# A hybrid decoder trunk on one core: the program issued in the order of its own list schedule

## The chip, the cores and the metric

The kernel runs on one core of a Trainium2 chip. The metric is the device time of one execution in microseconds. The kernel before took 1468.79 us, the median of three runs (1468.52 to 1474.27).

## The reference

Two layers on a sequence of 1024 rows and a width of 1024, in float32. Layer A is differential attention, layer B stick-breaking attention; each mixer's output is multiplied by a SiLU gate before its output projection, and added to the residual.

```
def _diff_attention(...):            # layer A, 8 heads, causal
    def probs(qb, k):
        s = einsum('bhqd,bshd->bhqs', qb, k) * scale
        return softmax(where(mask, s, -inf))
    a = probs(qb1, k1) - lam * probs(qb2, k2)
    return einsum('bhqs,bshe->bhqe', a, v)

def _stick_breaking(q, k, v):        # layer B, 16 heads of 64
    z = einsum('bhqd,bshd->bhqs', qb, k) * scale
    log_beta = log_sigmoid(z)
    log_1mb = where(mask, log_sigmoid(-z), 0.0)
    suffix = cumsum(log_1mb, reverse=True) - log_1mb
    a = where(mask, exp(log_beta + suffix), 0.0)
    return einsum('bhqs,bshe->bhqe', a, v)

x = x + (rms(diff_attention(...)) * (1 - lambda_init) * silu(g)) @ w_out      # layer A
x = x + (stick_breaking(...) * silu(g)) @ w_out                               # layer B
```

## The kernel before, in words

Every projection runs as three matmuls, because each operand is split into a high and a low part: high x high, high x low, low x high (L223 to L225; names `ah`/`al` for activations, two `w` tiles for weights). `group` (L211 on) makes such a projection in steps; a projection is 256 or 512 columns wide and accumulates into a PSUM tile `proj`, of which there are two.

Layer A treats its heads one after the other, layer B pairs of heads. For a head the program makes the projections of q, k, v and the gate; `scores` (L257 on) makes one visit of `sc` (one buffer of two banks, 64-row matmuls) for one or two blocks of 128 query rows; a chain on VectorE and ScalarE turns each score row tile `zl` into weights (layer A: L671 to L687; layer B: L855 copy, L857 mask on GpSimd, L867, two activations, L870, the scan L872, L873); `transposed` (L303 on) transposes them in TensorE into `tr` (three buffers), ScalarE copies that to `th` (L319), VectorE writes the rest to `tl` (L320), and the `av` matmuls read `th` and `tl` (L702 to L704, L888, L889) into the one `av` buffer, which L712 or L894 and L895 empty.

While head h is in its attention, the projections of head h+1 fill TensorE: `merge` interleaves the two lists of steps by their weights in the program's text. During layer A the weights of layer B are also converted and written back to DRAM: `park` (L178 on) loads a 256 KB `raw` tile, ScalarE makes `ph` from it (L186, L189), VectorE the rest (L187, L190), and two DMAs store them. At the start, `norm_rows` (L125 on) normalizes each of eight blocks of 128 rows: a Square with a sum on ScalarE (L129), some short instructions, a scale on VectorE (L131), eight transposes (L136), and the split into `ah` and `al` (L140, L141); the weights of the first head are split beside it (L162 to L165). Sixteen warm-up matmuls (L110) stand in front.

The order in which instructions reach each engine's queue is not that of the text. The tile framework collects them, and places them by a list schedule of its own with a timing model of the simulator; `hp()` puts an instruction ahead of all others, `later()` 400 places back. Each engine then works its queue strictly in order and waits on semaphores, and all DMAs of the kernel stand in the one queue of SyncE. The order is asked for in one line:

```
    with tile.TileContext(nc, schedule_with_timeline_sim=True) as tc:
        build(tc, args, out)
```

Of the kernel before, what the change touches and what calls it, by code (L numbers as in the profile page):

```python
# [34 lines left out]

def build(tc, ins, out):
    nc = tc.nc
    act, dve, pool, pe = nc.scalar, nc.vector, nc.gpsimd, nc.tensor
# [16 lines left out]
    layer_pool = lctx.enter_context(tc.tile_pool(name="la", bufs=1))  # L55
    def hp(k="hpe"):
# [5 lines left out]
    act.preload_act_table_set("natural_log_exp_and_others")  # L62
# [5 lines left out]
    layer = [layer_pool, 0]  # L68

    def T(tag, shape, bufs, dt=F32, pool=None):  # L70
        n_t[0] += 1
        return (pool or sb).tile(shape, dt, tag=tag, bufs=bufs, name=f"{tag}_{n_t[0]}")

    def PS(tag, bufs):
        n_t[0] += 1
        return ps.tile([P, 512], F32, tag=tag, bufs=bufs, name=f"{tag}_{n_t[0]}")
# [16 lines left out]
    def C(name, shape, dt=F32):  # L93
        return cp.tile(shape, dt, name=name)
# [3 lines left out]
    make_identity(nc, ident)  # L98
    eps = C("eps", [P, 1])
    dve.memset(eps, EPS)  # L100
    ones = layer_pool.tile([P, P], F32, name="ones")
    pool.memset(ones, 1.0 / P)
    mask_a = layer_pool.tile([P, HALF], mybir.dt.bfloat16, name="mask_a")
# [42 lines left out]
    def split_w(dst, src, gain=None):  # L146
# [3 lines left out]
        with hp("hpw") if len(started) > 1 else ExitStack():  # L150
            raw = T("raw", [P, HALF], B["raw"], pool=layer[0]) if started else T("o", [P, HALF], B["o"])
            r3 = raw.rearrange("p (k n) -> p k n", k=k)
            nc.sync.dma_start(raw if len(src.shape) == 2 else raw.rearrange("p (k n) -> p k n", k=src.shape[1]), src)
# [24 lines left out]
    def park(src, gain, dst):  # L178

        with later():  # L180
# [3 lines left out]
            nc.sync.dma_start(raw, src)  # L184
# [6 lines left out]
            for i, t in enumerate((f32(h), raw)):  # L191
                nc.sync.dma_start(dst(i), t.rearrange("p (j n) -> p j n", j=2))

    def w_parked(src):

        ws = [w_slots(4, 256) for _ in range(2)]
        for g in range(2):
            for i in range(2):
                nc.sync.dma_start(f32(ws[g][i]).rearrange("p k n -> p (k n)"), src[i, :, g * 1024:(g + 1) * 1024])
# [11 lines left out]
    def group(n, pairs, done):  # L211
# [45 lines left out]
    def scores(hd, visit, evac):  # L257

        first = True
        n_t[0] += 1  # L260
        pts = ps.tile([P, 2, 512], F32, tag="sc", bufs=1, name=f"sc_{n_t[0]}")
        col = 0
        for i, off, w in visit:
            rs_ = slice((i % 4) * P, (i % 4) * P + P)
            q, wm = hd.q[i // 4], max(w, 256)
# [698 lines left out]
```

## Time and profile before

| | |
|---|---|
| median of three runs | 1468.79 us |
| the profiled execution | 1470.76 us |
| its span, first to last instruction | 1469.0 us |
| granted TensorE clock, mean | 0.988 |
| PE busy | 1392.2 us |
| DVE, ACT, POOL busy | 1072.0, 908.8, 303.3 us |

PE is TensorE, DVE VectorE, ACT ScalarE, POOL GpSimd, SP the queue that issues DMAs. A matmul's end is modelled, so PE counts as busy while one is in its pipeline. Length less PE busy is the time in which TensorE did nothing. The granted clock is a share of 2.4 GHz; the engine has two levels, 1.2 and 2.4, so a share between them is a mixture. An instruction's idle time is the gap on its engine before it, and the name behind the arrow is what ended the gap.

### The profile page before, as it was taken

To read this page: it belongs to the slowest core of one execution; us is meant where nothing else is said; L and a number is where in the kernel's file an instruction comes from. 1 tells how busy PE (TensorE), PEld (TensorE's weight loads), DVE (VectorE), ACT (ScalarE), POOL (GpSimd) and SP (SyncE) were. 2 spreads that over 40 slices of the span, in tenths; PEclk is the share of its full clock that TensorE was granted. 3 is DMA by queue.
4 is the path that set the end of the run, shared out by engine and by line. 5 is a ranking of instruction groups with operands and counts; after the bars stand their busy time and mean duration, and the time that the engine had idled before them with its cause. 6 is when DMAs were issued, how large, how long until landed. Compare 5 with 4: busy or idle time off the path is not lost.

```text
span 1469.0 us, 24737 instructions
## 1 busy us (share of the span) xinstructions
PE 1392.2 (95%) x8944; PEld 1172.3 (80%) x8944; DVE 1072.0 (73%) x2145; ACT 908.8 (62%) x1834; POOL 303.3 (21%) x545
## 2 busy tenths in 40 slices
PE   8999999999989897899999999999999999988899
PEld 8888888888878786779987877777777877777799
DVE  8677787888777867886425786877878686788851
ACT  7666666666656656554226677768677676787610
POOL 0102112111221212110002232223314242334200
PEclk9999999999999999999999999999999999999999
DMA  5156555546455625351522122111212121253624
GB/s 202 62 161 209 155 193 185 169 151 212 151 172 172 194 83 190 112 205 73 179 73 87 63 68 63 69 58 63 80 58 87 58 87 58 72 194 137 229 84 147
DMA packets 94602, 185.93 MB, mean 127 GB/s; under 512 B 8720, under 2 KB 43792, under 8 KB 93456
## 3 DMA queue, kind: packets, MB, share of 16 engines
q1 hardware_dynamic: 94480, 184.35, 37.6%
q8 instruction: 71, 1.16, 0.3%
q14 instruction: 51, 0.42, 0.1%
HBM read 119.31 MB, written 65.01 MB: 125 GB/s over the span
## 4 chain that ended last, share of the span: by engine, by line
PE 40%; DVE 24%; ACT 13%; issue 11%; DMA 8%; POOL 2%; SPq 0%; ACTq 0%; DVEq 0%; POOLq 0%
PE proj L223 10%; PE proj L224 9%; PE proj L225 9%; DVE u4k L872 6%; DVE u4k L870 4%; PE tr L313 3%; PE sc L269 2%; ACT u4k L868 2%; DVE u4k L867 2%; DVE tl L320 2%; ACT u4k L869 2%; DVE zl L671 2%; ACT zl L682 2%; PE av L888 2%; DMA w_kv<-raw 1%
## 5 line engine op out<-in xcount | busy, mean ns | idle before, releaser
L223 PE MATMUL proj<-ah,w 128*128 128x512 f32 x768 | 309.9, 404 | 0.0
L225 PE MATMUL proj<-ah,w 128*128 128x512 f32 x768 | 308.0, 401 | 0.0
L224 PE MATMUL proj<-al,w 128*128 128x512 f32 x768 | 307.6, 400 | 0.0
L223 PE MATMUL proj<-w,ah 128*128 128x256 f32 x992 | 284.3, 287 | 9.5 <-ACT qk L610 6.2
L224 PE MATMUL proj<-w,ah 128*128 128x256 f32 x992 | 280.8, 283 | 0.0
L225 PE MATMUL proj<-w,al 128*128 128x256 f32 x992 | 280.7, 283 | 0.0
L223 PEld LDWEIGHTS proj<-w,ah 128*128 128x128 f32 x992 | 187.9, 189 | 18.4 <-ACT qk L610 8.4
L224 PEld LDWEIGHTS proj<-w,ah 128*128 128x128 f32 x992 | 188.0, 189 | 3.2 <-issue 2.5
L225 PEld LDWEIGHTS proj<-w,al 128*128 128x128 f32 x992 | 187.7, 189 | 1.9 <-issue 1.8
L872 DVE TENSOR_TENSOR_SCAN u4k<-zl,u4k 128x768 f32<-128x768 f32 (+4 forms) x96 | 182.1, 1903 | 1.2
L320 DVE TENSOR_TENSOR tl<-tr,th 128x512 fp32r<-128x512 f32 (+1 forms) x240 | 146.4, 628 | 43.3 <-ACT th L319 38.6
L225 PEld LDWEIGHTS proj<-ah,w 128*128 128x128 f32 x768 | 144.7, 188 | 35.3 <-issue 5.5
L223 PEld LDWEIGHTS proj<-ah,w 128*128 128x128 f32 x768 | 144.6, 188 | 34.2 <-issue 4.9
L224 PEld LDWEIGHTS proj<-al,w 128*128 128x128 f32 x768 | 144.9, 189 | 32.5 <-issue 4.2
L269 PE MATMUL sc<-kh,q 64*128 64x512 f32 (+2 forms) x768 | 141.3, 385 | 11.6 <-DVE small L671 10.6
L313 PE MATMUL tr<-ident,zl 128*128 128x128 f32 x864 | 131.3, 279 | 19.9 <-DVE tl L320 12.0
L873 ACT ACTIVATE zl<-u4k 128x768 f32<-128x768 f32 (+4 forms) x96 | 81.3, 846 | 107.4 <-DVE u4k L872 83.2
L857 POOL TENSOR_SCALAR_AFFINE_SELECT zl<-zl 128x128 f32<-128x128 f32 (+1 forms) x96 | 92.8, 980 | 236.6 <-ACT zl L855 223.3
L319 ACT ACTIVATE th<-tr 128x512 fp32r<-128x512 f32 (+1 forms) x240 | 126.3, 553 | 24.0 <-PE tr L313 17.3
L313 PEld LDWEIGHTS tr<-ident,zl 128*128 128x128 f32 x864 | 101.6, 143 | 38.9 <-DVE tl L320 18.3
L870 DVE SCALAR_TENSOR_TENSOR u4k<-zl,u4k 128x768 f32<-128x768 f32 (+4 forms) x96 | 94.1, 997 | 48.2 <-ACT u4k L869 47.7
L682 ACT ACTIVATE zl<-zl,small 128x256 f32<-128x256 f32 (+7 forms) x128 | 98.0, 768 | 29.2 <-DVE small L681 20.7
(150 smaller groups left out, 2547.0 us busy)
## 6 DMA issues: line engine op xcount, KB each, us to landing
w<-w_kv SPq DMA_DIRECT2D x32, 512.0 KB, 5.2
w<-w_b SPq DMA_DIRECT2D x32, 512.0 KB, 5.0
w<-w_o SPq DMA_DIRECT2D x24, 512.0 KB, 4.9
raw<-in_w_kv_dram SPq DMA_DIRECT2D x32, 256.0 KB, 2.9
w_kv<-ph SPq DMA_DIRECT2D x32, 256.0 KB, 3.1
w_kv<-raw SPq DMA_DIRECT2D x32, 256.0 KB, 3.4
raw<-in_w_b_dram SPq DMA_DIRECT2D x32, 256.0 KB, 3.0
w_b<-ph SPq DMA_DIRECT2D x32, 256.0 KB, 3.0
```

Of the source, the lines that this page charges most:

```text
L223: pe.matmul(box["p"], lh, rh, start=(j == 0), stop=False)
L224: pe.matmul(box["p"], lh, rl, start=False, stop=False)
L225: pe.matmul(box["p"], ll, rh, start=False, stop=last)
L269: pe.matmul(pts[:, c, col:col + wm], q[a][HI[c], rs_], hd.k[b][HI[c], off:off + wm], start=(a + b == 0), stop=(a == 1))
L313: pe.transpose(pt[:, o:o + P], a[:, (2 * t + b) * P:(2 * t + b + 1) * P], ident)
L319: act.activation(th[:, skip:], pt[:, skip:], AF.Copy)
L320: dve.tensor_tensor(tl[:, skip:], pt[:, skip:], f32(th[:, skip:]), ALU.subtract)
L682: act.activation(p[c][:, :n], p[c][:, :n], AF.Exp, bias=b, scale=-1.0, accum_out=s[:, c:c + 1])
L857: pool.affine_select(t3[:, :, n - P:], t3[:, :, n - P:], [[0, len(cs)], [-1, P]], ALU.is_ge, -BIG, base=-1, channel_multiplier=1)
L870: dve.scalar_tensor_tensor(u, zc, 0.0, u, ALU.min, ALU.subtract)
L872: dve.tensor_tensor_scan(ur, t[:, 1:w2 + 1][:, ::-1], ur, 0.0, ALU.add, ALU.subtract)
L873: act.activation(zc, u, AF.Exp, scale=-1.0)
```

## The change

The calls to the engines no longer go to the framework at once. `Order` records each with its engine, its operands and a duration from a table (`cost`), and at the end `issue` runs a list schedule: whenever an engine is free it takes the ready instruction of the lowest priority number (the place in the text; `hp()` goes ahead of all, `later()` 400 places back), if the buffers that it needs are free. The framework then only gets the instructions in that order. The three matmuls of a projection step, and all matmuls of one score visit, are recorded as one entry (`together`). Which instructions there are, their operands and the buffers are unchanged. All instructions carry the line of the one place that issues them, L374.

```
+class L:                                   # an operand: a tile and the part of it that is used
+    def part(self):
+        if self.root.space == "dram":
+            return self.box or [(0, n) for n in self.root.shape]
+        lo, hi = int(self.idx.min()), int(self.idx.max()) + 1
+        if self.root.space == "psum":
+            return [(lo // 512, (hi + 511) // 512)]
+        return [self.p, (lo, hi)]
...
+    def add(self, eng, method, a, kw):
+        took, lag = self.cost(eng, method, a, kw)
+        if eng == "pe" and not self.cur and a[1].p[1] - a[1].p[0] == 64:
+            took += 0.42
...
+            op.prio = i - 10 ** 9 if self.shift is None else i + self.shift
...
+        for x, w in [(x, False) for x in ins] + [(x, True) for x in outs]:
+            r, part = x.root, x.part()
+            for other, opart in (r.writes + r.reads if w else r.writes):
+                if other is not op and all(p[0] < q[1] and q[0] < p[1] for p, q in zip(part, opart)):
+                    op.deps.add(other)
...
+    def cost(self, eng, method, a, kw):
...
+        if eng == "pe":
...
+            t = {512: 0.228, 384: 0.172, 256: 0.12}[n]
+            return (t / 2, 0.17) if a[1].p[1] - a[1].p[0] == 64 else (t, 0.17)
...
+        if eng == "act":
+            by = isinstance(kw.get("scale"), L)
+            return (0.18 if by else 0.08) + (0.00078 if psum else 0.00086) * n + (0.19 if "accum_out" in kw else 0), 0.17
+        if eng == "dve":
+            if method == "tensor_tensor_scan":
+                return 0.06 + 0.0021 * n, 0.15
...
+        size = (k.p[1] - k.p[0]) * int(np.prod(k.idx.shape)) * 4
+        return 0.07, size / 180e3
...
+    def issue(self, prepare):
...
+                    op.at, free[e] = now, now + op.took
+                    if e == "sp":
+                        dma = max(now + 1.2, dma) + op.lag
+                        end = dma + 0.8
+                    else:
+                        end = free[e] + op.lag
...
+        with self.tc.manual_schedule():
+            for op in order:
...
+                e = self.real[op.eng]
+                for method, a, kw in op.calls:
+                    getattr(e, method)(*[real(x) for x in a], **{k: real(v) for k, v in kw.items()})
...
-    act, dve, pool, pe = nc.scalar, nc.vector, nc.gpsimd, nc.tensor
+    rec = Order(tc, {"pe": nc.tensor, "act": nc.scalar, "dve": nc.vector, "pool": nc.gpsimd, "sp": nc.sync})
+    act, dve, pool, pe, sp = (rec.engine(e) for e in ("act", "dve", "pool", "pe", "sp"))
...
     def hp(k="hpe"):
-        return tc.high_priority(offset=None if B[k] < 0 else B[k])
+        return rec.priority(None)
 
     def later():
-        return tc.high_priority(offset=-B["late"])
+        return rec.priority(B["late"])
...
-                pe.matmul(box["p"], lh, rh, start=(j == 0), stop=False)
-                pe.matmul(box["p"], lh, rl, start=False, stop=False)
-                pe.matmul(box["p"], ll, rh, start=False, stop=last)
+                with rec.together():
+                    pe.matmul(box["p"], lh, rh, start=(j == 0), stop=False)
+                    pe.matmul(box["p"], lh, rl, start=False, stop=False)
+                    pe.matmul(box["p"], ll, rh, start=False, stop=last)
...
+    rec.issue(prepare)
```

Three places show what moved. The first is ScalarE's queue in layer A, where the q and k projections of head 6 (of 0 to 7) begin: `ph` is a conversion of a parked weight, `qk` the evacuation of a projection. Before:

```order
L189 ACTIVATE ph_5819<-raw_5818,cols 128x512
L710 ACTIVATE t1k_4975<-tr_4977,eps 128x256
L291 ACTIVATE q_965_5036<-tr_5031,cols 128x512
L711 ACTIVATE t1k_4975<-t1k_4975 128x256
L291 ACTIVATE kh_5013<-tr_5040,cols 128x512
L189 ACTIVATE ph_5871<-raw_5870,cols 128x512
L610 ACTIVATE qk_5812<-proj_5787 128x256
L319 ACTIVATE th_5178<-tr_5174 128x384
L189 ACTIVATE ph_5937<-raw_5936,cols 128x512
L189 ACTIVATE ph_6042<-raw_6041,cols 128x512
L610 ACTIVATE qk_5812<-proj_5841 128x256
L707 ACTIVATE t1k_5190<-av_5173 128x256
```

and now, from shortly after the first `qk` evacuation of that head to the third:

```order
L374 ACTIVATE th_5819<-tr_5781 128x512
L374 ACTIVATE o_5826<-g2k_5716 128x512
L374 ACTIVATE o_5826<-o_5826 128x512 x2
L374 ACTIVATE qk_5788<-proj_5790 128x256
L374 ACTIVATE w_5753<-raw_5772,cols 128x256 x2
L374 ACTIVATE g1k_5868<-qk_5788 128x256
L374 ACTIVATE th_5874<-tr_5845 128x512
L374 ACTIVATE w_5882<-raw_5778,cols 128x256 x2
L374 ACTIVATE th_5897<-tr_5857 128x512
L374 ACTIVATE w_5882<-raw_5832,cols 128x256 x2
L374 ACTIVATE ph_5937<-raw_5880,cols 128x512
L374 ACTIVATE qk_5788<-proj_5864 128x256
```

Before, four conversions stand in ten rows, two of them straight in front of a `qk` evacuation; now one does, and the rows between are splits of the next weights, copies of transposes and the gate.

The second is TensorE's queue at the start. Each pair of `tr` rows is one block of x's rows (blocks 0 and 1 before; 0 is not repeated below), `proj` the first projection, of block 0. Before:

```order
L136 MATMUL tr_126<-ident,zl_112 128x128 x4
L136 MATMUL tr_133<-ident,zl_112 128x128 x4
L223 MATMUL proj_460<-w_140,ah_105 128x256
L224 MATMUL proj_460<-w_141,ah_105 128x256
L136 MATMUL tr_184<-ident,zl_170 128x128 x4
L136 MATMUL tr_191<-ident,zl_170 128x128 x4
L225 MATMUL proj_460<-w_140,al_106 128x256
L223 MATMUL proj_460<-w_140,ah_105 128x256
L224 MATMUL proj_460<-w_141,ah_105 128x256
L225 MATMUL proj_460<-w_140,al_106 128x256
```

and now, from the first projection on (`proj_195` is of block 0, `proj_245` of block 1):

```order
L374 MATMUL proj_195<-w_166,ah_182 128x256
L374 MATMUL proj_195<-w_171,ah_182 128x256
L374 MATMUL proj_195<-w_166,al_189 128x256
L374 MATMUL tr_224<-ident,zl_210 128x128 x4
L374 MATMUL tr_232<-ident,zl_210 128x128 x4
L374 MATMUL proj_245<-w_166,ah_182 128x256
L374 MATMUL proj_245<-w_171,ah_182 128x256
L374 MATMUL proj_245<-w_166,al_189 128x256
L374 MATMUL tr_263<-ident,zl_228 128x128 x4
L374 MATMUL tr_275<-ident,zl_228 128x128 x4
L374 MATMUL tr_286<-ident,zl_251 128x128 x4
L374 MATMUL tr_296<-ident,zl_251 128x128 x4
```

Before, the rest of block 0's projection follows the transposes of block 1; now it follows those of block 3, and one triple of block 1 has moved ahead of blocks 2 and 3.

The third is TensorE's queue in layer B, from the last transpose of a group to the `av` matmuls that read it. Before (the `av` matmul that reads this group stands 14 projection matmuls and one score group behind the last row):

```order
L313 MATMUL tr_11726<-ident,zl_11467 128x128
L313 MATMUL tr_11742<-ident,zl_11390 128x128
L313 MATMUL tr_11742<-ident,zl_11468 128x128
L313 MATMUL tr_11742<-ident,zl_11390 128x128
L313 MATMUL tr_11742<-ident,zl_11468 128x128
L313 MATMUL tr_11771<-ident,zl_11390 128x128
L313 MATMUL tr_11771<-ident,zl_11468 128x128
L313 MATMUL tr_11771<-ident,zl_11390 128x128
L313 MATMUL tr_11771<-ident,zl_11468 128x128
L223 MATMUL proj_11797<-ah_8570,w_11203 128x512
L224 MATMUL proj_11797<-al_8571,w_11203 128x512
L225 MATMUL proj_11797<-ah_8570,w_11204 128x512
```

and now:

```order
L374 MATMUL tr_11832<-ident,zl_11263 128x128
L374 MATMUL sc_11836<-kh_10440,q_2108_10962 128x256 x2
L374 MATMUL sc_11836<-kl_10457,q_2108_10962 128x256 x2
L374 MATMUL sc_11836<-kh_10440,q_2109_10970 128x256 x2
L374 MATMUL sc_11836<-kh_10440,q_2108_10962 128x256 x2
L374 MATMUL sc_11836<-kl_10457,q_2108_10962 128x256 x2
L374 MATMUL sc_11836<-kh_10440,q_2109_10970 128x256 x2
L374 MATMUL av_11706<-th_11799,v_10775 128x256
L374 MATMUL proj_11795<-ah_8729,w_11152 128x512
L374 MATMUL proj_11795<-al_8740,w_11152 128x512
L374 MATMUL proj_11795<-ah_8729,w_11155 128x512
L374 MATMUL av_11706<-tl_11806,v_10775 128x256
```

The `av` matmul that reads `th` now stands one score group behind the transposes, and the one that reads `tl` a projection triple behind that.

## Rows read from the trace of the kernel before

**Rows 1.** The page, busy time of each engine: us (share of the span) x instructions.
```profile
PE 1392.2 (95%) x8944; PEld 1172.3 (80%) x8944; DVE 1072.0 (73%) x2145; ACT 908.8 (62%) x1834; POOL 303.3 (21%) x545
```

**Rows 2.** Busy time by stretch; columns: length, PE, PEld, DVE, ACT, POOL, PEclk, DMA, GB/s.
```profile
0.00:560.00 560.00, 537.24 (x3619) 464.62 (x3620) 427.38 (x1141) 361.30 (x842) 95.95 (x149) 0.99 0.51 165
560.00:605.00 45.00, 33.22 (x215) 25.60 (x214) 38.93 (x102) 26.52 (x59) 14.12 (x19) 0.92 0.51 176
605.00:745.00 140.00, 136.82 (x1042) 125.85 (x1041) 92.76 (x249) 61.24 (x137) 6.60 (x21) 1.00 0.39 134
745.00:1200.00 455.00, 443.22 (x2436) 347.32 (x2435) 327.88 (x402) 311.48 (x538) 122.73 (x238) 1.00 0.22 71
1200.00:1311.00 111.00, 101.71 (x574) 80.27 (x574) 86.66 (x111) 78.85 (x143) 35.55 (x64) 0.97 0.24 86
1311.00:1402.00 91.00, 76.11 (x529) 65.01 (x528) 80.34 (x105) 66.00 (x113) 27.64 (x52) 0.94 0.50 180
1402.00:1469.00 67.00, 63.85 (x542) 63.62 (x540) 18.03 (x40) 3.40 (x8) 0.71 (x4) 1.00 0.35 126
```

**Rows 3.** Waits of PE, whole span: waiting, releaser, us in total, times, longest.
```profile
PE tr L313 <- DVE tl L320: 12.0, 8, 4.0
PE av L888 <- DVE o L895: 11.0, 13, 2.7
PE sc L269 <- DVE small L671: 10.6, 10, 2.4
...
PE proj L223 <- ACT qk L610: 6.2, 7, 1.7
```

**Rows 4.** Waits of ACT in 0 to 600 us.
```profile
ACT ph L189 <- DMA raw<-in_w_kv_dram: 21.7, 17, 3.5
ACT ph L189 <- DMA raw<-in_w_b_dram: 17.9, 13, 3.6
```

**Rows 5.** Timeline of ACT from 420 us: start, length, instruction, idle before and releaser.
```profile
420.26 0.72 ACT L189 ACTIVATE ph<-raw,cols 128x512 fp32r<-128x512 f32 x1 [3.54 <-DMA raw<-in_w_b_dram]
420.89 0.36 ACT L610 ACTIVATE qk<-proj 128x256 f32<-128x256 f32 x1
```

**Rows 6.** The page, DMA issues: count, KB each, us to landing.
```profile
raw<-in_w_b_dram SPq DMA_DIRECT2D x32, 256.0 KB, 3.0
```

**Rows 7.** Timeline of ACT in the first 30 us.
```profile
6.22 2.51 ACT L164 ACTIVATE w<-o,cols 128x256 fp32r<-128x256 f32 x6 [0.28 <-DMA o<-in_w_qk_dram]
8.77 1.06 ACT L129 ACTIVATE zl<-kl 128x1024 f32<-128x1024 f32 x1
```

**Rows 8.** Timeline of PE in the first 30 us.
```profile
10.15 1.97 PE L136 MATMUL tr<-ident,zl 128*128 128x128 f32 x8 [2.09 <-DVE small L118]
...
12.64 1.50 PE L136 MATMUL tr<-ident,zl 128*128 128x128 f32 x8
13.90 0.36 PE L225 MATMUL proj<-w,al 128*128 128x256 f32 x1
...
23.11 1.03 PE L136 MATMUL tr<-ident,zl 128*128 128x128 f32 x8
```

**Rows 9.** Groups by shape: instruction, count, busy us, mean ns, idle before and releasers.
```profile
L320 DVE TENSOR_TENSOR tl<-tr,th 128x512 fp32r<-128x512 f32 x144 | 95.9, 683 | 26.6 <-ACT th L319 22.3 <-issue 3.1 <-PE tr L313 0.8
...
L320 DVE TENSOR_TENSOR tl<-tr,th 128x384 fp32r<-128x384 f32 x96 | 51.7, 546 | 16.8 <-ACT th L319 16.3
...
L319 ACT ACTIVATE th<-tr 128x512 fp32r<-128x512 f32 x144 | 82.1, 594 | 12.9 <-PE tr L313 8.5 <-PE av L888 2.3 <-POOL o L246 1.3
...
L872 DVE TENSOR_TENSOR_SCAN u4k<-zl,u4k 128x768 f32<-128x768 f32 x24 | 45.0, 1876 | 0.5
...
L872 DVE TENSOR_TENSOR_SCAN u4k<-zl,u4k 128x640 f32<-128x640 f32 x16 | 32.9, 2083 | 0.0
...
L867 DVE TENSOR_SCALAR u4k<-zl 128x896 int32<-128x896 int32 x16 | 16.2, 1049 | 4.5 <-ACT zl L855 4.4
...
L867 DVE TENSOR_SCALAR u4k<-zl 128x768 int32<-128x768 int32 x24 | 12.9, 538 | 6.6 <-POOL zl L857 6.6
```

More of the change, by code (lines that the diff above doesn't have):

```diff
@@ L1 @@
+import heapq
 import math
@@ new lines, in _rearranged, with groups @@
+def _rearranged(idx, pat, kw):
+    def groups(s):
+        out_, cur = [], None
+        for t in s.replace("(", " ( ").replace(")", " ) ").split():
+            if t == "(":
+                cur = []
+            elif t == ")":
+                out_.append(cur)
+                cur = None
+            elif cur is None:
+                out_.append([t])
+            else:
+                cur.append(t)
+        return out_
+    a, b = (groups(s) for s in pat.split("->"))
+    assert a[0] == b[0] == ["p"]
+    a, b = a[1:], b[1:]
+    size, names = dict(kw), []
+    for g, n in zip(a, idx.shape):
+        known = int(np.prod([size[t] for t in g if t in size]))
+        for t in g:
+            if t not in size:
+                size[t] = n // known
+        names += g
+    x = idx.reshape([size[t] for t in names])
+    order = [t for g in b for t in g]
+    return x.transpose([names.index(t) for t in order]).reshape([int(np.prod([size[t] for t in g])) for g in b])
@@ L66, in build, with fixed, kept @@
     n_w = [0]
-    layer = [layer_pool, 0]
+    layer = ["la", 0]
     def T(tag, shape, bufs, dt=F32, pool=None):
         n_t[0] += 1
-        return (pool or sb).tile(shape, dt, tag=tag, bufs=bufs, name=f"{tag}_{n_t[0]}")
+        pool, name = pool or "sb", f"{tag}_{n_t[0]}"
+        return L(Root(shape, dt, "psum" if pool == "ps" else "sbuf", pool, slot=(pool, tag), bufs=bufs,
+                      make=lambda: pools[pool].tile(shape, dt, tag=tag, bufs=bufs, name=name)))
     def PS(tag, bufs):
-        n_t[0] += 1
-        return ps.tile([P, 512], F32, tag=tag, bufs=bufs, name=f"{tag}_{n_t[0]}")
+        return T(tag, [P, 512], bufs, pool="ps")
+    def fixed(pool, shape, dt, name):
+        return L(Root(shape, dt, "sbuf", pool, real=pools[pool].tile(shape, dt, name=name)))
+    def kept(shape, name):
+        return L(Root(shape, F32, "dram", "dr", real=dr.tile(shape, F32, name=name)))
     zt = lambda: T("zl", [P, S], B["al"], pool=layer[0])
@@ L93, in C @@
     def C(name, shape, dt=F32):
[L94 removed]
+        return fixed("cp", shape, dt, name)
     ident = C("ident", [P, P])
[L98 removed]
+    make_identity(nc, ident.real())
     eps = C("eps", [P, 1])
     dve.memset(eps, EPS)
[L101 removed]
+    ones = fixed("la", [P, P], F32, "ones")
     pool.memset(ones, 1.0 / P)
[L103 removed]
+    mask_a = fixed("la", [P, HALF], mybir.dt.bfloat16, "mask_a")
     pool.memset(mask_a, 0.0)
@@ L805, in build, with prepare @@
               OutProj(ins["a_w_out"], og_a, x_in, heads_a, sink_a, {0: (0, D)}), (0, 1), extra)
-    lctx.close()
-    layer[1] = 1
-    layer[0] = lctx.enter_context(tc.tile_pool(name="lb", bufs=1))
+    layer[:] = ["lb", 1]
+    def prepare():
+        if "lb" not in pools:
+            lctx.close()
+            pools["lb"] = lctx.enter_context(tc.tile_pool(name="lb", bufs=1))
     def qkv_b(p):
```

295 lines of the change are left out of this document (256 added, 39 removed).

## The prediction, made before the changed kernel ran

> **What bounds the kernel now.** First the engines' totals [rows 1]: TensorE is busy 95% of a span of 1469.0 us, VectorE 73%, ScalarE 62%. An order can win only what TensorE stands still or runs slow, so the second view is the table of stretches [rows 2]. Length less PE busy is idle time: 22.8 us in 0 to 560 (layer A, heads 0 to 6), 11.8 in 560 to 605 (its last head), 3.2 in 605 to 745, 11.8 in 745 to 1200 (layer B, steady), 9.3 in 1200 to 1311, 14.9 in 1311 to 1402 (layer B's last heads), 3.1 in the tail: 76.8 in all. Where it idles the granted clock is under 1: 0.99, 0.92, 0.97 and 0.94. One less that share, times the length, is 5.6 + 3.6 + 3.3 + 5.5 = 18 us lost to time at 1.2 instead of 2.4 GHz. The two make 95 us, and start and end (about 7) stay, so 1380 is the least that reordering can reach.
>
> Third, what ended TensorE's waits [rows 3]: no DMA is among the releasers. It waits for ScalarE and VectorE to empty or fill a tile: `tl` 12.0 us, `o` 11.0, the row minima behind the scores 10.6, `qk` 6.2. Fourth, why those are late in layer A: ScalarE itself waits for loads of weights that it converts for layer B, 21.7 and 17.9 us [rows 4]. The stretch at 416 to 421 us shows how one becomes the other [rows 5]: conversion `ph` of L189 heads ScalarE's queue, its data arrive 3.54 us later, and only behind it comes L610, for which TensorE stands. In layer B the late ones are VectorE's, which works 80.3 of 91 us in the last stretch [rows 2].
>
> **The change part by part.** Instructions and their durations are the same on every engine; only places in the five queues change. I go stretch by stretch.
>
> Layer A, steady: 22.8 idle, of which about 4 is the first wait for data, leaving 18.8. The old order put four `ph` conversions into ten rows of ScalarE, around the first `qk` evacuations of a head; the new one has a single one in the twelve rows that hold the second and third (the first place shown). The cost table gives a 256 KB load 1.2 + 262,144 / 180,000 + 0.8 = 3.5 us and makes transfers queue behind each other; the trace has 3.0 from issue to landing [rows 6]. So a conversion is placed when its data are there, and what was a blocked queue becomes a few us of ordinary waits. I take back 15 of 18.8; bounds: 0 (the waits only move) and 18.8.
>
> Layer A, last head: 11.8 idle. Little filling work is left, and in the new order some score groups still stand directly behind one another. A score tile has one buffer, and two evacuations of 128x512 stand between two groups (`th` has the same form and takes 0.59 us [rows 9]), so with hand-overs about 1.5 us of idle each, some four times. I take back 5; bounds 0 and 8.
>
> Layer B, steady: 11.8 idle. At the third place shown the old order leaves 17 projection matmuls and more between a transpose and the first `av` matmul that reads it; the new one leaves a score group, and one projection triple between the readers of `th` and of `tl`. That costs nothing if ScalarE and VectorE are on time (0.59 + 0.68 us for the two halves [rows 9], 1.3 to 1.6 with hand-overs), and it gives buffers back earlier. The table is right for most shapes but not all: it has 0.06 + 0.0021 x 640 = 1.40 us for the scan of 640, the trace 2.08 [rows 9]. The extra 0.68 x 16 = 11 us falls on an engine that is 72% busy here. I take back 6; bounds 11.8 and a loss of 32 (in this layer 8 pairs x 2 heads x 10 groups = 160 hand-overs, each 0.2).
>
> A row speaks against any table with one time for one instruction: L867 takes 1.05 us on 896 elements and 0.54 on 768 [rows 9], so it is delayed by something beside its size. The Trainium skill, "SBUF — State Buffer", section Who interferes with whom, says that a VectorE `tensor_scalar` in a two-port mode and a GpSimd instruction exclude each other for the whole instruction, and that the order of issue decides who blocks; no row shown here proves that GpSimd is the cause. By the rule the delays depend on what meets what, so the plan cannot hold them and new meetings may be worse. By the rows, 16 x (1.05 - 0.63) = 7 us is lost on 896 elements today; if it vanished or doubled, VectorE would change by 7 us either way, mostly beside TensorE's work.
>
> Layer B, last heads: 9.3 + 14.9 = 24.2 idle. The new order also has score groups back to back here (about five times 1.5 us) and some close `av` matmuls: some 10 us that are sure to be idle, and I add 5 for lateness. So I take back 9; bounds 0 and 14.
>
> The start: here the change costs. In the old order the projection of the first row-block runs from 13.90 on, between the transposes of the blocks behind it [rows 8]. In the new one, after one triple for block 0 and one for block 1, all other projection work stands behind the transposes of blocks 2 and 3. The cause is in the list's own books: `part` describes a tile's part by its lowest and highest element, so a write of one row-block into eight chunks of `ah` covers the other row-blocks' chunks too, and a projection seems to need all four blocks. On ScalarE, block 1's Square moves behind block 0's two evacuations and five conversions. Walked with rows: warm-ups end at 10.15 - 2.09 = 8.06, block 0's transposes run to about 10.0, the evacuations to 10.7, five conversions at 2.51 / 6 = 0.42 [rows 7] to 12.8. Block 1's Square starts there instead of 8.77, and its transposes follow 12.64 - 8.77 = 3.9 later, at 16.7 instead of 12.64. Blocks 2 and 3 pass the same chain, 3 to 4 us each: the projection resumes at about 23.5. Until 23.11 the old order had done 23.11 - 13.90 - 1.0 = 8.2 us of projection [rows 8], the new one 0.7. So 7.5 us are lost, and about 0.5 for a clock that falls meanwhile. I take 8; bounds 3 (less waits between blocks) and 12.
>
> The clock: it falls where TensorE waits, so I return it in proportion, 11 of 18; bounds 0 and 15.
>
> The sum: -15 - 5 - 6 - 9 - 11 + 8 = -38. The profiled execution took 1470.8 (span 1469.0), 2 us above the median of 1468.8 of the three runs, so 1433 in its own terms and 1431 against the median.
>
> **The rivals.** One: the plan is nearly met on the chip. The waits outside start, end and the sure ones of the last heads (about 16) vanish, and the clock comes back nearly in full: -76.8 + 7 + 16 - 16 + 8 = -62, so about 1407. For it: the table's values fit most rows. Against it: 640 and 896.
>
> Two: waits only move. Layer A gives back 10, the clock 4, layer B nothing, the start costs 8: -6, about 1463. For it: VectorE is at 80 of 91 us where the idle time is worst, and no order makes that less work.
>
> Three, slower: thin hand-overs in layer B. `tl` is made 240 times (144 + 96 [rows 9]). 17 matmuls of 512 columns at 2.4 GHz are 3.6 us, so the old order hides a lateness of about 2 us beside the hand-over's 1.6; the new one, with one triple of projections between, passes most of it on. A scan lasts 1.9 to 2.1 us [rows 9], so a `tl` that misses its slot waits up to that long. If every fourth of the 240 misses by 0.9 us, 54 us come in; with the start's 8 and the other gains' 46 the sum is +16, about 1485; with 1.2 us it is +34. It decides from a mean loss of 38 / 240 = 0.16 us per hand-over on.
>
> That the change leaves the order as it was can be excluded: the three places show it.
>
> **How the numbers follow.** The forecast (1410 to 1455, likeliest 1431) gets 0.45; the plan met (under 1410) 0.14; waits that move (1455 to 1476) 0.23; thin hand-overs (above 1476) 0.18. About 0.5%, 7.3 us, is what a measurement of this kernel tells from no change: faster means below 1461.4, slower above 1476.1. Faster takes the first two and half of the third, 0.71; same 0.12; slower 0.17. The range leaves out a tenth on each side: 1400 to 1483.
>
> **What would show it.** Right: PE idle in 0 to 560 falls under 10 us with ScalarE's waits for loads under 15; the idle at the end of layer B is near 15; the start shows transposes of four blocks with almost no projection before 22 us. Wrong: idle in the steady part of layer B above 25, ended by VectorE `tl` (rival three); the start's projection running before 17 us (the walk was wrong); or ScalarE waiting for `raw` as long as now (the table's transfers are no better).

## The result, and the profile after

The changed kernel takes 1488.2 us (median of 4 runs, 1485.4 to 1490.0), the kernel before in the same comparison 1470.0: a ratio of 1.0117, 95% interval 1.009 to 1.0145. It is 1.2% slower; the forecast was 1431 and the range ended at 1483. The profiled execution took 1487.9, its span is 1486.1. All its instructions carry L374, the line that issues the list, so groups are told by their tiles.

The engines' totals of the kernel after, to be held against [rows 1]:

```profile
PE 1403.6 (94%) x8944; PEld 1181.0 (79%) x8944; DVE 1080.6 (73%) x2145; ACT 920.8 (62%) x1834; POOL 299.3 (20%) x545
```

The same number of matmuls is busy 11 us longer, and idle grows from 76.8 to 82.5 us. The stretches of the kernel after (columns as in [rows 2]):

```profile
0.00:50.00 50.00, 39.80 (x236) 35.58 (x237) 31.40 (x96) 31.32 (x72) 1.85 (x11) 0.90 0.41 148
...
0.00:560.00 560.00, 527.19 (x3560) 453.51 (x3561) 444.39 (x1165) 366.00 (x847) 106.12 (x159) 0.99 0.48 154
560.00:615.00 55.00, 51.30 (x313) 40.54 (x312) 42.16 (x109) 33.31 (x76) 10.21 (x15) 1.00 0.57 197
615.00:705.00 90.00, 69.80 (x443) 61.03 (x442) 52.57 (x123) 29.86 (x60) 2.62 (x8) 0.83 0.41 141
705.00:760.00 55.00, 53.12 (x434) 51.71 (x433) 26.97 (x69) 16.24 (x33) 0.00 (x0) 1.00 0.30 101
760.00:1215.00 455.00, 446.25 (x2480) 351.81 (x2479) 327.55 (x428) 318.95 (x551) 121.41 (x244) 1.00 0.22 75
1215.00:1330.00 115.00, 112.05 (x656) 88.94 (x655) 90.89 (x115) 87.65 (x155) 34.15 (x74) 1.00 0.24 83
1330.00:1420.00 90.00, 80.91 (x554) 71.20 (x555) 81.02 (x108) 68.45 (x115) 24.82 (x48) 0.92 0.54 205
```

One row stands out: 615 to 705, the end of layer A, with 20.2 us idle and a clock of 0.83. Layer B's rows are all a little better than in [rows 2], the first 560 us are worse (32.8 idle against 22.8), 10.2 of the 32.8 in the first 50.

Idle time misses waits that end before the modelled end of the matmul ahead. So a second measure: lost time is the time passed less TensorE's own work, each matmul counted at the interval in which its form follows itself in the traces (0.234 us for 512 columns of projection, 0.118 for 256, 0.109 for a transpose of 128, and so on; 1293 us in all). It is counted up to the end of the last matmul, which comes 3.1 us before the end of either span, and time at the slower clock counts as lost. Both kernels do the same work, so stages can be cut at equal work; the 525 us mark is where the scores of layer A's last head begin in either kernel, 601.4 us into the span before and 602.3 after:

| TensorE's own work, us | before | after | change |
|---|---|---|---|
| 0 to 25, the start | 9.0 | 18.0 | +9.0 |
| 25 to 525, layer A, heads 0 to 6 | 68.5 | 62.4 | -6.1 |
| 525 to 600, layer A's last head and end | 7.2 | 40.2 | +33.0 |
| 600 to 1075, layer B | 40.9 | 37.9 | -3.0 |
| 1075 to 1225, layer B's last heads | 44.9 | 29.4 | -15.5 |
| rest | 2.2 | 1.8 | -0.4 |

The sum is +17.0, the spans differ by 17.1. The minus 6.1 is itself the sum of two opposite changes. Up to 502 us of work, which the old order reached at 560 us, heads 0 to 6 lose 48.8 us before and 60.5 after; from there to the last head it is 20.0 before and 2.3 after. The old order's 20.0 lie in 560 to 605, the second stretch of [rows 2], and the largest wait there is of scores for the row minima of the group before:

```profile
PE sc L269 <- DVE small L671: 6.0, 5, 2.4
```

The waits of TensorE in the kernel after, over the whole span, to be held against [rows 3]:

```profile
PE tr L374 <- DVE zl L374: 19.4, 11, 6.3
PE tr L374 <- POOL qk L374: 12.4, 16, 1.9
PE sc L374 <- DVE small L374: 9.6, 11, 1.4
PE sc L374 <- ACT zl L374: 6.7, 6, 1.9
PE av L374 <- DVE o L374: 5.9, 7, 1.4
PE av L374 <- DVE tl L374: 5.4, 14, 0.9
```

ScalarE's `qk`, which [rows 3] has as a releaser, is gone; VectorE's normalised rows `zl` and GpSimd's `qk`, 1.0 and 1.9 us before, now lead the list. The waits of ScalarE for the loads of [rows 4], same stretch, 0 to 600 us, after:

```profile
ACT ph L374 <- DMA raw<-in_w_b_dram: 1.6, 2, 0.9
ACT ph L374 <- DMA raw<-in_w_kv_dram: 0.8, 2, 0.6
```

From 39.6 to 2.4 us: the list did what was expected of it for the loads, and TensorE got little of it.

The start, TensorE after, against [rows 8]:

```profile
10.23 0.38 PE L374 MATMUL proj<-w,al 128*128 128x256 f32 x1 [0.22 <-DVE al L374]
15.22 1.94 PE L374 MATMUL tr<-ident,zl 128*128 128x128 f32 x8 [4.61 <-DVE zl L374]
...
20.35 3.71 PE L374 MATMUL tr<-ident,zl 128*128 128x128 f32 x16 [2.05 <-DVE small L374]
23.71 0.78 PE L374 MATMUL proj<-w,ah 128*128 128x256 f32 x2
```

These are the end of the first projection triple, block 1's transposes, after one more triple those of blocks 2 and 3, and the projection that resumes at 23.71; block 0's transposes stand before. Then the hole at the end of layer A, TensorE's rows with the longest waits after 640 us:

```profile
645.00 2.18 PE L374 MATMUL tr<-ident,zl 128*128 128x128 f32 x9 [3.23 <-DVE zl L374]
...
663.73 2.18 PE L374 MATMUL tr<-ident,zl 128*128 128x128 f32 x9 [6.26 <-DVE zl L374]
...
674.10 0.38 PE L374 MATMUL proj<-w,ah 128*128 128x256 f32 x1 [2.05 <-ACT w L374]
676.69 0.58 PE L374 MATMUL proj<-w,ah 128*128 128x256 f32 x1 [2.21 <-DVE w L374]
```

Two kinds stand there: the last rows' softmax (`zl`), with no projection beside it, and then projections whose weights `w` are not converted yet. The DMA queue at that place, after, tells why they are not:

```profile
615.86 0.33 SPq L374 DMA_DIRECT2D raw<-in_a_w_out_dram  x1
...
625.57 9.70 SPq L374 DMA_DIRECT2D raw<-in_b_w_out_dram  x3
...
666.23 0.38 SPq L374 DMA_DIRECT2D raw<-in_b_w_out_dram  x1
...
667.16 0.42 SPq L374 DMA_DIRECT2D raw<-in_a_w_out_dram  x1
```

`in_a_w_out` are the weights of layer A's output projection, the only filling work left; `in_b_w_out` are weights for layer B that are only converted and parked. Both go through the three `raw` buffers, which the list hands out in the order of the text. The parked ones, issued 400 places late by `later`, hold the buffers that the urgent ones wait for. The last of the three parked tiles issued from 625.57 on lands at 637.5 us, and ScalarE converts it at 665.16; between 615.86 and 667.16 no load of `in_a_w_out` is issued. The kernel before issued the last head's loads in that time:

```profile
620.80 10.57 SPq L153 DMA_DIRECT2D raw<-in_a_w_out_dram  x7
```

It had issued its first load of `in_a_w_out` at 504.6 us, the kernel after at 571.2. One thing beside the buffers stood in the way: the queue works in order, and from 642.1 to 657.5 its head, a load of x into `kh`, waited for score matmuls. No run took that load out of the way by itself.

### The profile page after: what moved, and what is told of

It is laid out like the page before. It is cut to its first block, busy times and chain, and to the rows that moved or that the text cites. A ratio compares the mean times of both kernels' runs of the same rounds, so it can differ in the third digit from the quotient of the medians.

```text
span 1486.1 us, 24678 instructions
## 1 busy us (share of the span) xinstructions
PE 1403.6 (94%) x8944; PEld 1181.0 (79%) x8944; DVE 1080.6 (73%) x2145; ACT 920.8 (62%) x1834; POOL 299.3 (20%) x545
## 4 chain that ended last, share of the span: by engine, by line
PE 29%; DVE 19%; ACT 9%; issue 3%; POOL 0%; DMA 0%; SPq 0%; DVEq 0%; ACTq 0%; POOLq 0%
PE proj L374 20%; DVE u4k L374 12%; PE av L374 4%; ACT u4k L374 3%; ACT zl L374 3%; PE tr L374 3%; DVE tl L374 2%; PE sc L374 2%; DVE zl L374 1%; DVE o L374 1%; ACT o L374 1%; DVE kl L374 1%; DVE v L374 1%; DVE g2k L374 1%; DVE small L374 0%
## 5 line engine op out<-in xcount | busy, mean ns | idle before, releaser
L374 PE MATMUL proj<-ah,w 128*128 128x512 f32 x1536 | 542.6, 403 | 0.0
L374 PE MATMUL proj<-w,ah 128*128 128x256 f32 x1984 | 382.0, 292 | 7.1 <-ACT w L374 2.7
L374 PEld LDWEIGHTS proj<-ah,w 128*128 128x128 f32 x1536 | 289.0, 188 | 69.6 <-issue 15.4
L374 PEld LDWEIGHTS proj<-w,ah 128*128 128x128 f32 x1984 | 313.9, 194 | 19.3 <-issue 5.8
L374 PE MATMUL proj<-al,w 128*128 128x512 f32 x768 | 300.2, 391 | 0.0
L374 PE MATMUL proj<-w,al 128*128 128x256 f32 x992 | 283.1, 285 | 0.2 <-DVE al L374 0.2
L374 PEld LDWEIGHTS proj<-w,al 128*128 128x128 f32 x992 | 192.3, 194 | 0.7 <-DVE al L374 0.7
L374 DVE TENSOR_TENSOR_SCAN u4k<-zl,u4k 128x768 f32<-128x768 f32 (+4 forms) x96 | 176.7, 1841 | 3.0
L374 PE MATMUL tr<-ident,zl 128*128 128x128 f32 x992 | 152.1, 284 | 22.7 <-DVE zl L374 19.4
L374 ACT ACTIVATE th<-tr 128x512 fp32r<-128x512 f32 (+1 forms) x240 | 126.4, 551 | 67.5 <-PE tr L374 64.5
L374 DVE TENSOR_TENSOR tl<-tr,th 128x512 fp32r<-128x512 f32 (+1 forms) x240 | 144.1, 628 | 32.7 <-ACT th L374 32.0
L374 PE MATMUL av<-th,v 128*128 128x256 f32 x640 | 155.0, 294 | 10.1 <-DVE o L374 5.9
L374 ACT ACTIVATE u4k<-u4k 128x768 f32<-128x768 f32 (+4 forms) x192 | 159.0, 843 | 7.3 <-DVE u4k L374 4.6
L374 PEld LDWEIGHTS proj<-al,w 128*128 128x128 f32 x768 | 144.9, 189 | 19.9
L374 PE MATMUL sc<-kh,q 64*128 64x512 f32 (+2 forms) x768 | 141.8, 387 | 16.4 <-DVE small L374 9.6
L374 PEld LDWEIGHTS tr<-ident,zl 128*128 128x128 f32 x992 | 119.7, 145 | 45.2 <-issue 21.3
L374 PE MATMUL av<-tl,v 128*128 128x256 f32 x480 | 135.4, 302 | 6.4 <-DVE tl L374 5.4
L374 PEld LDWEIGHTS av<-th,v 128*128 128x128 f32 x640 | 113.3, 193 | 29.6 <-issue 11.6
L374 POOL TENSOR_TENSOR o<-o,o 128x512 f32<-128x512 f32 (+1 forms) x56 | 87.9, 1570 | 186.1 <-DVE o L374 171.4
L374 ACT ACTIVATE zl<-zl,small 128x256 f32<-128x256 f32 (+7 forms) x128 | 98.2, 769 | 43.3 <-DVE small L374 43.3
L374 PEld LDWEIGHTS sc<-kh,q 64*128 64x128 f32 x768 | 70.3, 186 | 61.8 <-issue 19.1
L374 DVE SCALAR_TENSOR_TENSOR u4k<-zl,u4k 128x768 f32<-128x768 f32 (+4 forms) x96 | 94.1, 981 | 31.8 <-ACT u4k L374 31.2
```

The costliest lines, as they stand in the source:

```text
L374: getattr(e, method)(*[real(x) for x in a], **{k: real(v) for k, v in kw.items()})
```

## The experiments

Two theories for the hole: **loads** (filling work has no weights) and **chain** (scores start too late and the filling work is spent). For the rest: **thin hand-overs**, and the list's own books at the start. All times are medians, and the ratios are to the kernel before on the same chip. "Back" counts from 1488.2 us, measured in another round; the kernel before took 1470.0 to 1471.9 in the four rounds, so a difference across rounds is good to about 2 us.

**Parts.** The start alone.

```diff
-        return [self.p, (lo, hi)]
+        n = self.root.shape[-1]
+        row, col = self.idx // n, self.idx % n
+        return [self.p, (int(row.min()), int(row.max()) + 1), (int(col.min()), int(col.max()) + 1)]
```

> The changed kernel, with one thing mended: a tile's part is kept as a row range and a column range, not as lowest to highest element, so one row-block's write into ah no longer covers the others' chunks. If the start's loss comes from those books, the projection of block 0 resumes before 17 us instead of behind four blocks' transposes, and TensorE's busy time in 0 to 50 us rises from 39.8 to 44 or more; time 1488 less 5 to 8, 1480 to 1483. If the loss at the start has another cause (the loads of x, the clock), the start keeps its 39.8 and the time 1488. All theories leave the hole at 640 to 705 us where it is (21.9 us busy of 40 in its middle), at most a few us earlier; if that hole is set by loads that do not come earlier, part of the gain is given back there and the time falls by only 2 to 5.

1479.8 us, ratio 1.0061 (1.0044 to 1.0078): 8 back. The start loses 13.3 instead of 18.0, layer A 58.5 instead of 62.4, the hole stays (41.4). TensorE's busy time in 0 to 50 is 42.6, less than the 44 expected: one wait is left, behind block 1's normalisation:

```profile
9.97 0.38 PE L376 MATMUL proj<-w,al 128*128 128x256 f32 x1 [0.72 <-DVE al L376]
...
17.22 1.94 PE L376 MATMUL tr<-ident,zl 128*128 128x128 f32 x8 [4.17 <-DVE zl L376]
```

Projection fills 10 to 13 us now. The books were the cause of about half of the start's loss (4.7 of 9.0); what is left, 4.3, is about that one wait.

**Four buffers.**

```diff
-    B = {... "g2k": 3, ... "raw": 3, ...
+    B = {... "g2k": 2, ... "raw": 4, ...
```

> The changed kernel with four buffers for raw weights instead of three (g2k two instead of three, to make room). Theory loads: TensorE stands at 640 to 705 us because the next weights of layer A's output projection, the only filling work left, wait for a raw buffer behind parked conversions for layer B, which the list serves in text order; a fourth buffer brings those loads forward, the lost time there (33 us) falls by about 11, and the time is 1474 to 1480. Rival chain: TensorE stands for the softmax chain of the last rows with its filling work used up, loads play no part; time 1485 to 1490 and the same gaps. Rival hand-overs: the 1.2% are many small waits elsewhere; time 1485 to 1490.

1476.3 us, 1.0042 (1.0027 to 1.0056): 12 back. The profiled execution, at 1478.6, has 9 of them, and by place 8.9 are in the end of layer A (40.2 to 31.3), nothing in layer A's 500 us before (63.2).

**Four buffers, six heads.**

```diff
-            main = spread(main, extra[h * len(extra) // (n - 1):(h + 1) * len(extra) // (n - 1)])
+            main = spread(main, extra[h * len(extra) // (n - 2):(h + 1) * len(extra) // (n - 2)])
```

> As the kernel with four raw buffers, and the 80 parked conversions for layer B are spread over the first six heads' text instead of seven, so that none of them stands ahead of the weights of layer A's output projection. Theory loads: the hole at 640 to 705 us nearly closes, 24 to 28 of its 33 us come back and the time is 1458 to 1466, below the kernel before; waits of 2 to 8 us may appear at 350 to 600 us, since more conversions fall there. Rivals chain and hand-overs: the hole stays, 1485 or more, since neither the last softmax nor the steady hand-overs are touched.

1469.1 us, 0.999 (0.9978 to 1.0001): 19 back, less than the 22 to 30 expected. The end of layer A falls to 16.6, so 23.6 of its 33 us are gone; layer A before it rises to 68.1. Denser conversions there would explain the rise, but that is not shown: ScalarE waits for none of their loads in this kernel. The DMA queue shows the urgent loads early, in this kernel:

```profile
604.11 5.42 SPq L374 DMA_DIRECT2D raw<-in_a_w_out_dram  x4
```

**Control: the kernel before, four buffers** (the same edit as for the second experiment, made to the old kernel).

> The kernel before with the same two buffer counts (raw four, g2k two): a control, whether the buffer is worth something in any order. Theory loads: the old order already has the output projection's weights early (loads at 505 to 585 us), there is no hole to close, and only ScalarE's waits for loads in layer A shrink: 1462 to 1470. If it gains as much as the changed kernel does (10 us or more), the buffer is worth it whatever the order and says nothing on the cause.

1450.6 us, 0.9871 (0.9852 to 0.9891): 20 faster, against the expectation. So a faster time with four buffers says nothing by itself. The places do: here the gain is in layer A's heads 0 to 6 (68.5 to 41.1) and the end of the layer gets slower (7.2 to 13.5); in the changed kernel it is the other way round. Of the 27 us, 17 come from the stretch that was 560 to 605 (20.0 to 3.1) and 10 from the steady heads before it. ScalarE's waits for the loads of [rows 4] fall from 39.6 to 21.1 us with it. So 27 us is not what those waits cost the old order: in 560 to 605 its queue too has parked loads (562 to 570) between loads of `in_a_w_out` (561 to 585), and no run separates the two there.

**GpSimd's margin.**

```diff
-            return (0.13 + 0.0006 * n if method == "memset" else 0.1 + 0.0028 * n), 0.06
+            return (0.13 + 0.0006 * n if method == "memset" else 0.1 + 0.0028 * n), 1
```

> The changed kernel with one number of its table altered: a GpSimd instruction's result is counted as ready 1.0 us after its end instead of 0.06. In the steady part of layer A TensorE stands 12.1 us, 15 times, before the transposes of qk that GpSimd's four rope products release. Theory thin hand-overs in layer A: the list has other work for TensorE there but gives it the transposes at the moment the table thinks them ready; with the wider margin these waits fall under 3 us and the time to 1476 to 1481; the hole at 640 to 705 us stays. Rival contention: GpSimd is late because of what it meets, and TensorE then stands for the next thing in the same chain (scores behind their minima, av behind th and tl); the waits move, time 1485 to 1490.

1481.8 us, 1.0066 (1.0048 to 1.0083): 6 back, 0.8 us above the expectation. Both theories had a part of it: TensorE's 12.4 us behind GpSimd's `qk` are gone, but those behind `tl` rise from 5.4 to 7.6 and behind `th` from 3.8 to 7.5.

**All three mends** (parts, buffers, six heads).

> The row and column parts (start), four raw buffers, and the parked conversions in six heads' text, together. If the three places are independent, the gains add: 1488 less 8 for the start and 19 for the buffers and the spread, 1461, range 1457 to 1465, which is below the kernel before by 0.6%. If the gain at the start is given back in layer A, 1467 to 1470.

1463.0 us, 0.9937 (0.9922 to 0.9952), as expected: the totals add. Place by place they do not: the end of layer A loses 9.0, next to the old order's 7.2, but heads 0 to 6 lose 71.6, more than with either mend alone (58.5 and 68.1).

**All three, wider margins.** The second number that the table's function returns, how long after an instruction its result counts as ready:

```diff
         took, lag = self.cost(eng, method, a, kw)
+        if eng == "dve":
+            lag = 0.45
...
-            return (0.18 if by else 0.08) + (0.00078 if psum else 0.00086) * n + (0.19 if "accum_out" in kw else 0), 0.17
+            return (0.18 if by else 0.08) + (0.00078 if psum else 0.00086) * n + (0.19 if "accum_out" in kw else 0), 0.47
...
-            return (0.13 + 0.0006 * n if method == "memset" else 0.1 + 0.0028 * n), 0.06
+            return (0.13 + 0.0006 * n if method == "memset" else 0.1 + 0.0028 * n), 0.6
```

> The same three, and wider margins in the table: results count as ready 0.6 us (GpSimd), 0.47 (ScalarE) and 0.45 us (VectorE) after the end instead of 0.06, 0.17 and 0.15. Theory thin hand-overs in layer A: the steady part of layer A loses 42 us over the matmuls' own time between the 25th and the 375th microsecond of TensorE's work, 16 more than in the old order; the margin takes back 12 to 25, time 1438 to 1452. Rival: the margins only make the plan longer where chains bound it (starts, ends, layer B), time 1458 to 1470.

1407.3 us, 0.9559 (0.954 to 0.9577): 56 less than without the margins, and 31 to 45 below what was expected. The expectation counted layer A alone. Layer A falls from 71.6 to 45.6, but layer B too, from 38.2 to 22.9, and its last heads from 29.9 to 21.8. TensorE's idle time falls from 67.4 to 33.9 us (1460.5 - 1393.1 and 1406.3 - 1372.4), its busy time by 20.7 at the same mean clock of 0.994. Totals and largest waits without the margins:

```profile
PE 1393.1 (95%) x8944; PEld 1170.8 (80%) x8944; DVE 1087.7 (74%) x2145; ACT 921.1 (63%) x1834; POOL 299.3 (20%) x545
```

```profile
PE tr L376 <- POOL qk L376: 13.5, 15, 1.8
PE sc L376 <- DVE small L376: 8.5, 13, 1.2
PE tr L376 <- DVE zl L376: 7.9, 7, 4.2
PE av L376 <- DVE tl L376: 7.6, 15, 1.2
```

and with them:

```profile
PE 1372.4 (98%) x8944; PEld 1169.6 (83%) x8944; DVE 1088.5 (77%) x2145; ACT 918.3 (65%) x1834; POOL 291.7 (21%) x545
```

```profile
PE sc L378 <- DVE small L378: 6.6, 7, 2.2
PE av L378 <- DVE tl L378: 6.1, 12, 1.4
PE tr L378 <- DVE zl L378: 3.8, 3, 2.5
PE sc L378 <- ACT zl L378: 2.8, 2, 1.7
PE tr L378 <- POOL qk L378: 2.3, 5, 0.7
```

By the kind of step (start to start, less the first matmul's own interval), what is lost going from a projection matmul to a transpose falls from 26.9 to 7.1 us, from a projection to an `av` matmul from 21.1 to 8.7: the places where the list takes TensorE off filling work because, by the table, a result is ready.

**Scores first.**

```diff
-                main[i][1]()
+                with rec.priority(keep[0]):
+                    main[i][1]()
...
+        keep[0] = (0 if layer[1] else -300)
         op.open_rows(f0, True)
```

> The changed kernel with the score and softmax steps of layer A's last head put 300 places earlier in the list's priorities, so that they go ahead of the output projection's filling work. Rival chain: the hole at 640 to 705 us comes from scores that start too late, with the filling work spent before them; then 10 us or more come back, 1478 or less. Theory loads: the filling work that is left has no weights at that time and nothing changes, 1485 to 1491.

1477.1 us, 1.0032 (1.002 to 1.0043): 11 back, where the theory of loads alone expected none. The end of layer A falls from 40.2 to 27.4, and TensorE's waits in 560 to 720 us of this kernel are now

```profile
PE proj L374 <- ACT w L374: 8.6, 1, 8.6
PE tr L374 <- DVE zl L374: 4.6, 3, 3.6
```

ScalarE makes that `w` right after a load of `in_a_w_out` lands (issued at 663.97, landed at 666.92; TensorE goes on at 667.63). So the hole is both: with the chain earlier, TensorE stands for the weights. Neither theory alone holds.

**Margins alone**, on the changed kernel as it is.

> The changed kernel with the wider margins alone (results ready 0.6, 0.47 and 0.45 us after the end of GpSimd's, ScalarE's and VectorE's instructions); three raw buffers, seven heads' text and the old parts stay. Theory thin hand-overs: together with the three other edits the margins gave 56 us (1463 to 1407). If they act by themselves, the steady parts of both layers give back the same 40 or so here; the hole at the end of layer A stays or grows by up to 15, so 1440 to 1458: the change would have been faster than the kernel before with nothing but other margins. If they only work once the loads are early, 1475 or more.

1446.4 us, 0.9841 (0.9822 to 0.986): 42 back with three numbers of the table (41 by the ratios). Start (17.8) and end of layer A (44.0) are as bad as before; layer A loses 40.4 and layer B 23.2. In the list a result that counts later also frees its buffers later, so a margin moves both; no run separates the two.

**VectorE's margin alone**, with the three mends (0.15 to 0.45).

> Parts, four raw buffers and six heads, and the wider margin for VectorE alone (0.45 us instead of 0.15). In the kernel with those three edits and narrow margins TensorE's waits end with VectorE's results for about 30 us, with GpSimd's for 13.5, with ScalarE's for about 12. If each engine's margin takes back its own releases, about half of the 56 us comes, 1432 to 1442. If a margin on one engine only shifts the wait to the next link of the chain, 1450 to 1463.

1436.9 us, 0.9777 (0.9758 to 0.9796): 26 of the 56, as expected of each engine's own releases.

**ScalarE's margin alone**, with the three mends (0.17 to 0.47).

> The same three edits, and the wider margin for ScalarE alone (0.47 us instead of 0.17). ScalarE ends only about 12 us of TensorE's waits, but its results feed VectorE's (th before tl, Exp before the normalisation). Each engine for itself: 1449 to 1456. If ScalarE's hand-over to VectorE is where the chains are late first: 1425 to 1440, and the waits that VectorE ends shrink as well.

1443.7 us, 0.9824 (0.9804 to 0.9844): 19 of the 56, between the two expectations. The waits that VectorE ends do not shrink; in this kernel one of them is the largest:

```profile
PE av L376 <- DVE tl L376: 20.6, 18, 1.4
```

So a margin takes back its own engine's releases, and another engine's stand out. 26 + 19 leave about 10 for GpSimd's if they add, or 15 by the ratios (24 and 17 of 56); GpSimd's margin alone was not run with the mends.

**Wider still**, with the three mends: 0.7 us for ScalarE and VectorE, 1.0 for GpSimd.

> The same three edits, and margins of 1.0 us (GpSimd) and 0.7 us (ScalarE, VectorE). If the lateness that the narrow margins missed lies under 0.3 us, nothing more is to be had in the steady parts and the list, which must now leave TensorE idle in places at 400 to 650 us, gets longer: 1412 to 1422. If lateness reaches 0.5 us and more, time falls below 1403.

1401.4 us, 0.9535 (0.9517 to 0.9554), the fastest of all, 4.7% below the kernel before. Layer A falls on to 37.5, the other stages stay (7.0, 24.3, 20.8). That is what was expected if lateness in layer A reaches 0.5 us; the step from the narrower margins is 6 us in time and 3.5 by the ratios, so it is small.

## Why the prediction was wrong

**Layer A, last head: the sum had no term for it, and it lost 33.** This step alone turns the sign: without it the change would measure 17 - 33 = -16 us. The prediction took 560 to 605 for the last head and counted minus 5 there. By the count of score matmuls, 72 to a head, that stretch holds the end of head 6 (of 0 to 7). The last head's scores run from 601.4 on, in the stretch of [rows 2] with 3.2 us idle, to which the sum gave nothing, neither gain nor loss. The prediction did say that little filling work is left at the end, but it priced only short gaps between score groups, some four of 1.5 us. It did not ask which weights the filling work needs and what stands ahead of their loads. The loads of `in_a_w_out` behind the parked ones are an order in the DMA queue, as plain as the three places that it did compare. Four buffers took back 9 us in that stage, buffers and text together 24, the earlier scores 13; no other single edit took back over 2.

**Layer A, heads 0 to 6: minus 20 became minus 6, and not for the reason given.** Two terms belong here, minus 15 for 0 to 560 and the minus 5 for 560 to 605. Loads no longer block ScalarE (39.6 to 2.4 us, under the 15 named), and TensorE's 6.2 us behind `qk` are gone: that part of the mechanism was right. But in the steady heads the loss did not fall, it rose, by the equal work from 48.8 to 60.5 us, and idle in 0 to 560 is 32.8 us, not under 10. What brought the minus 6 is the old order's 20.0 us in 560 to 605, of which 2.3 are left. The "few us of ordinary waits" are the step that failed. Start to start, less the first matmul's own interval, TensorE loses 10.5 us in this stage before, in going from projections or scores to a transpose and from projections to an `av` matmul; after it loses 24.2, and with margins alone 10.4. With margins alone the stage loses 40.4 in place of 62.4. Layer B is alike: minus 3 where 6 was forecast, and minus 18 with margins.

**The cause, thin hand-overs,** was seen, as rival three, and put in one place only. (Its 17 projection matmuls take 4.0 us by the interval of 0.234, not 3.6; nothing here hangs on that.) It was to cost 54 us more than the old order's in layer B; the mark named for it, idle above 25 in layer B's steady part, did not come (8.8). Its time, about 1485, came true by luck: the hole at the end of layer A made it. Where the new order is worse by thin hand-overs is layer A. In layer B's last heads it is the old order that loses more by them (14.1 us in going from projections to transposes and `av` matmuls, the new one 4.5), so over the whole span the step from projection to `av` looks alike (15.2 and 16.9) while the step from projection to transpose does not (11.9 and 25.5). By the run with margins alone the planned times cost the new list about 41 us, the largest term of all, in three of the five stages. What margins would give the old order was not run.

**The reason given for it was wrong.** The prediction held the table's 1.40 us for a scan of 640 against the trace's 2.08 [rows 9] and called the table wrong. That 2.08 is a mean of two kinds, seven of 1.46 to 1.48 us and nine of 2.52 to 2.59. In the trace after the same scans take:

```profile
L374 DVE TENSOR_TENSOR_SCAN u4k<-zl,u4k 128x640 f32<-128x640 f32 x16 | 23.9, 1491 | 0.5
...
L374 DVE TENSOR_SCALAR u4k<-zl 128x896 int32<-128x896 int32 x16 | 9.9, 632 | 6.3 <-POOL o L374 5.8 <-ACT zl L374 0.5
```

The next VectorE instruction starts 1.41 after a scan's start (median of 16). The table is right for an undisturbed instruction, and for the hand-over as well: a `th` of 512 elements lasts 0.593 us, follows itself after 0.48, and TensorE, where it waits for ScalarE, starts 0.053 after the end (median of the 23 waits over 0.15 us before). That is 0.17 beyond the interval, the table's number. A table that is right in the middle has no room for scatter. That scatter is what the margins cover is argued, not shown: no run removed it.

**The start: right.** Plus 9.0 for plus 8, the projection at 23.71 for 23.5, and the cause named first, the list's books, confirmed for about half of the loss.

**Layer B's last heads: right in the sum.** Minus 9 and a share of the clock, 11 x (3.3 + 5.5) / 18 = 5, make minus 14; measured -15.5. The parts fit less well: idle fell by 12.2, from 24.2 to 12.0 us in 1215 to 1420 (the mark was near 15), and the clock gave back 1.6, 8.8 less (1 - 0.92) x 90 = 7.2.

**The clock** was to give back 11 us and took some 10 more: the mean granted clock fell from 0.988 to 0.981, so one less that share, times the span, rose from 17 to 28 us. It fell where TensorE waits, as the prediction has it, and the waits moved. In 615 to 705 the granted clock is 0.83, a mixture of the levels 1.2 and 2.4 GHz, and TensorE stood up to 6.26 us at a time there; (1 - 0.83) x 90 = 15 us of the 40 lost there are slow time.

## What to carry to other kernels

A list schedule whose times are right in the middle still puts every consumer at the moment its data should be there; where other work is at hand, plan results late by a few tenths of a microsecond (0.3 to 0.54 us more gave 41 to 56 us here, a further 0.23 to 0.4 some 5). Read for each stretch what filling work is left and follow its loads back to the buffer they wait for: a buffer handed out in text order lets a deferred, unimportant load hold up an urgent one. Before a stretch gets a name and a term, count its instructions: 560 to 605 was not the last head. And when an order is compared with an old one, look at what both lose, not at their difference alone.

## What the runs showed of the hardware that was not expected

TensorE's busy time is no constant of its instructions: 1403.6, 1393.1, 1372.4 and 1367.4 us for the same 8944 matmuls in the kernel after, with three mends, with margins and with the widest. In the second and the third the mean granted clock is 0.994. A matmul's end is modelled, so a wait shorter than its modelled tail counts as busy.

The long instructions of [rows 9] moved with the order. Before, 9 of the 16 scans of 640 were longer than 1.59 us, each with a GpSimd product of two tiles beside it, and the five longest `tensor_scalar` of 896 elements (1.71 to 2.07 us) had one too. After, none of those scans is long and the longest `tensor_scalar` of 896 takes 0.71; now five scans of 1024, single ones of other sizes and six `tensor_scalar` of 768 (1.08 to 1.28, each beside GpSimd's `o<-g2k,o`) are long. The Trainium skill, "SBUF — State Buffer", section Who interferes with whom, says besides the rule that the prediction cites that a VectorE instruction with two inputs in SBUF contends with a GpSimd instruction that reads SBUF; a scan has two. The trace before agrees in the main: of 14 scans of 640 elements or more beside a GpSimd product of two tiles 12 were 0.5 to 1.1 us longer than is usual for their size, of 40 beside an affine select 12 were 0.1 to 0.2 us longer, of 26 beside a memset or nothing none. What decided beside a product was the start. In all 19 cases of the two traces (12 before, 7 after) in which the product was running when the scan began, the scan was lengthened. In all 10 (2 and 8) in which the scan began first it kept its time, and the product ended 1.09 to 1.10 us after the scan and took 1.7 to 3.1 us, where 1.3 is usual. No run here took GpSimd away.
